# Differential attention: whole-tile splits of queries and keys, and query low parts moved by transfers

## The chip, the cores and the metric

The kernel runs on one core of a Trainium2 chip. The metric is the device time of one execution in microseconds (us). The kernel before has a median of 1926.02 us over three runs (1925.98 to 1927.47).

## The reference, cut to what matters

The reference is a decoder trunk of two layers over 512 tokens of width 1024, in float32. Each layer is: a half-step SwiGLU feed-forward, a token mixer, a cross attention into 256 memory tokens, and a second half-step feed-forward, each followed by a layer norm. The mixer of the first layer is differential attention, and the change lies in it:

```python
def diff_attention(x, w_qkv, w_o, lam_q, lam_k, subln_g, cos, sin, lam_init):
    q, k, v = jnp.split(x @ w_qkv, 3, axis=-1)
    q = q.reshape(B, S, H, 2, dk)          # 8 heads, each with 2 components of 64
    k = k.reshape(B, S, H, 2, dk)
    v = v.reshape(B, S, H, 2 * dk)
    q = rope(q, c5, s5)
    k = rope(k, c5, s5)
    ...
        s = jnp.einsum('bqhcd,bkhcd->bhcqk', qblk, k) * scale     # scale = 64 ** -0.5
        s = jnp.where(mask, s, jnp.finfo(jnp.float32).min)
        p = jax.nn.softmax(s, axis=-1)
        a = p[:, :, 0] - lam * p[:, :, 1]
        return jnp.einsum('bhqk,bkhe->bqhe', a, v)
    ...
```

Each head has two components. Each component has its own scores, from 64 columns of the query and 64 of the key; the two softmaxes are combined and multiplied with one value matrix of 128 columns.

## The kernel before

**Products in parts.** The operands of TensorE are of the type float32r, a rounded float32. To keep the reference's precision, the kernel splits a float32 operand x into a high part hi = round(x), written by ScalarE as float32r, and a low part lo = x - hi, written by VectorE. A product of two operands is then hi·hi + hi·lo + lo·hi, three matmuls in one accumulation (`mm3`, lines 201 to 208).

**The stage.** `diff_attention` (line 1205) runs in one phase. A main generator, `da_main`, goes through the heads in pairs: values of the pair, and for each head the projection of the query and of the key, 24 matmuls of 128x512 each. A side generator, `da_side`, does the attention of the heads whose query and key are ready: scores and masked exponential (`da_scores`), combination of the two softmaxes (`da_mix`), transposes of the result (`da_turn`), product with the values (`da_out`), norm and transposes of the output. `weave` (line 210) interleaves both in program order by estimated TensorE time; the scores of a head enter once the main work has gone 6000 ns past its key. From this order a planner, which walks the program with its own estimates of durations, sets the order of instructions on each engine; within an engine the order is then fixed, and an instruction that waits holds all those behind it on that engine. The DMA issues of SP are such a queue too: weight loads (L233, L266, L300) wait there for one of two raw buffers to come free.

**Rope.** A projection's result lies in PSUM with its 128 rows on the partitions: component 0 on the partitions 0 to 63 and component 1 on 64 to 127. These are the two `HALVES`. `da_rope` (L1025) takes two temporaries t1 and t2 of the tag `rt`, which has two buffers. VectorE shuffles partitions into t2 (L1028), multiplies the PSUM tile with the cosines into t1 (L1029), POOL multiplies t2 with the sines (L1030), and VectorE adds (L1031). The result t is t1.

**The query before** (`da_query`, L1034). For each component m there is one tile q[m] of the tag `qk`. ScalarE writes the scaled high part of component m in its own half (L1041). VectorE writes the low part of the same component in the other half (L1042). So q[m] holds high part over low part, 64 partitions each.

**The key before** (`da_key`, L1047). For each component, ScalarE writes the high part in its half (L1055), VectorE the low part in the same half of a tile of `low_keys` (L1056), whose other half was set to zero at the start of the stage (L1209), and ScalarE copies the high part into the other half (L1057).

**Scores before** (`da_scores`, L1060). The first product (L1070) multiplies q[m] with the doubled high key, which gives hi·hi + lo·hi in one matmul. The second (L1071) multiplies the same q[m] with the low key that is zero in one half, which gives hi·lo. So two matmuls per component replace three.

**Buffers.** The tag `qk` has 8 buffers (four tiles for each of two heads), `low` has 4 (a pair for each of two heads, taken in turn), `rt` 2, `raw` 2 (line 1577). PSUM tiles of the projections have two banks in turn, which come free when L1028 and L1029 have read them. At the end of the stage, free `qk` and `low` buffers take the split output weights (L1217).

Of the kernel before, what the change touches and what calls it, by code (L numbers as in the profile page):

```python
# [9 lines left out]
F32 = mybir.dt.float32  # L10
F32R = mybir.dt.float32r
I32 = mybir.dt.int32
AF = mybir.ActivationFunctionType
ALU = mybir.AluOpType
# [15 lines left out]
DA_DK = 64  # L30
# [10 lines left out]
HALVES = (slice(0, DA_DK), slice(DA_DK, P))  # L41
# [58 lines left out]
def drain(units):  # L100
    for _ in units:
        pass
# [7 lines left out]
class Trunk:  # L110
# [75 lines left out]
    def mm(self, name):  # L186
        return self.mmp.tile([P, S], F32, tag="mm", name=name)
# [846 lines left out]
    def da_query(self, ps):  # L1034

        nc, t = self.nc, self.da_rope(ps)
        got = [self.act("qk") for m in range(2)]
        scale = DA_DK**-0.5
        for m, q in enumerate(got):
            here, there = HALVES[m], HALVES[1 - m]  # L1040
            nc.scalar.activation(q[here], t[here], AF.Copy, scale=scale)  # L1041
            nc.vector.scalar_tensor_tensor(  # L1042
                q[there], t[here], scale, q[here].bitcast(F32), ALU.mult, ALU.subtract
            )
        return got

    def da_key(self, ps):  # L1047


        nc, t = self.nc, self.da_rope(ps)  # L1050
        his, los = [self.act("qk") for m in range(2)], self.low_keys[len(self.heads) % 2]
        for m in range(2):
            here, there = HALVES[m], HALVES[1 - m]
            hi, lo = his[m], los[m]
            nc.scalar.copy(hi[here], t[here])  # L1055
            nc.vector.tensor_sub(lo[here], t[here], hi[here].bitcast(F32))  # L1056
            nc.scalar.copy(hi[there], hi[here].bitcast(F32))  # L1057
        return his, los

    def da_scores(self, st, i):  # L1060

        nc = self.nc
        q, k, n = st["q"], st["k"], (i + 1) * P
        qi, kn = slice(i * P, n), slice(0, n)
        mx, rc, cf = self.small("mx"), self.small("rc", (P, 1)), self.small("cf", (P, 1))
        sm = st["sm"][:, i]
        sc = [self.aux("sc")[:, :n] for m in range(2)]
        mm = nc.tensor.matmul
        for m in range(2):
            mm(sc[m], q[m][:, qi], k[0][m][:, kn], start=True, stop=False)  # L1070
            mm(sc[m], q[m][:, qi], k[1][m][:, kn], start=False, stop=True)  # L1071
        p = [self.tmp("p")[:, :n] for m in range(2)]
        with self.tc.high_priority():
            for m in range(2):
                least = mx[:, m : m + 1]
                nc.vector.tensor_tensor_reduce(
                    p[m], sc[m], self.mask[:, S - n :], -1.0, -NEG, ALU.add, ALU.min, least
                )
                nc.scalar.activation(
                    p[m], p[m], AF.Exp, bias=least, scale=-1.0, accum_out=sm[:, m : m + 1]  # L1080
                )
        st["m", i] = p, sm, rc, cf
# [120 lines left out]
                yield W_E[1]  # L1203

    def diff_attention(self, layer, ln):
        self.low_keys = [self.pair("low") for i in range(2)]
        for pair in self.low_keys:
            for m, t in enumerate(pair):
                self.nc.gpsimd.memset(t[HALVES[1 - m]].bitcast(F32), 0.0)  # L1209
        self.mask = self.act("mask", (P, S), mybir.dt.bfloat16)  # L1210
        self.nc.gpsimd.memset(self.mask[:, : S - P], 0.0)
        self.nc.gpsimd.tensor_copy(self.mask[:, S - P :], self.maskr)
        self.heads, self.oT = [], [None] * DA_H
        self.weave(self.da_main(), self.da_side(), GAP)
        self.begin_ln(layer, ln, 1.0)
        home = lambda tag: lambda: self.pair(tag)
        homes = [[home("qk")] * 4, [home("low"), home("low"), home("p"), home("p")]]  # L1217
        drain(self.to_tokens(self.oT[4:], self.a["da_w_o"][0], 4, 4, False, True, ALPHA, homes))
# [355 lines left out]

    def mixer(self, layer, ln):
        if layer == 0:
            bufs = dict(low=4, rt=2, a=4, p=6, o=2, qk=8, _x=0, v=4, oT=11, mask=1)
            with self.other_pools(), self.phase_pool(("v", "v"), "rt", **bufs):
                self.diff_attention(layer, ln)
            self.close_side()  # L1580
        else:
            self.later = ExitStack()
            self.later.enter_context(self.stage_pools(4, dict(raw=2), ("wh", "wl", "mem", "p", "raw")))
            self.to_w(self.later)
            self.kvp = self.later.enter_context(self.pool("kv"))
            bufs = dict(p=4, pw=1, gb=2, _x=0, pooled=16, sq=1)
            with self.phase_pool(("gb", "gb"), "sq", **bufs):
                side = self.pool_mixer(layer, ln)
                with self.tc.high_priority():
                    self.load_memory()  # L1590
                w = self.a["xa_wkv"][layer]
                raws = [self.raw_cols(w, c) for c in (0, D)]
                self.pool_bias()
                next(side)
                self.kv, self.keys, self.kv_bufs = [], [], 10
                self.weave(self.early_kv(layer, ln, 2, raws), side, 850, 8500)
            self.close_side()
# [46 lines left out]
```

## Time and profile before

| what | value |
|---|---|
| median of three runs | 1926.02 us |
| the profiled execution | 1925.08 us |
| its span, first to last instruction | 1923.3 us |
| granted TensorE clock | 0.999 |
| the attention stage in it | about 340 to 550 us |

All times in rows of the profile are from the profiled execution, counted from the start of its span. PE is TensorE's matmuls, PEld its weight loads, DVE is VectorE, ACT ScalarE, POOL GpSimd and SP the engine whose queue issues transfers; PEld and SP with a "q" behind them are sequencers. A group's row gives line, engine, operation, output<-inputs, shapes and count; then busy us and the mean ns of one; then the idle time of the engine just before, with what ended it. A row in order of time gives start, duration (us), engine, line and operation. A row of waits gives who waited <- for whom: us in total, times, longest. Matmuls overlap each other in their pipeline, so that a busy TensorE is not one at its peak rate. Releasers are inferred.

### The profile page before, as it was taken

The numbers are of one execution on the slowest core, as the hardware profiler recorded it, in microseconds if no ns is written. First come the engines' busy times: TensorE is split into PE (matmuls) and PEld (weight loads), VectorE is DVE, ScalarE is ACT, GpSimd is POOL, SyncE is SP. The second block draws the span as 40 slices with busy tenths as digits, with TensorE's granted clock in tenths as the row PEclk, the third lists the DMA queues.
The fourth block names the chain that finished last, engine by engine and source line by source line (L and its number), as shares of the span: only waits on it lengthen the run. The fifth ranks groups of instructions, "written<-read, shape, count | busy, mean of one in ns | idle before, by whom it ended". The sixth has DMA issues, their size and how long they took to land.

```text
span 1923.3 us, 32450 instructions
## 1 busy us (share of the span) xinstructions
PE 1892.8 (98%) x13050; PEld 1737.6 (90%) x13050; DVE 1563.6 (81%) x2263; ACT 1023.1 (53%) x1580; POOL 319.7 (17%) x278
## 2 busy tenths in 40 slices
PE   8999999999999999999999999999999999999998
PEld 7999998888878888999998999999899889999997
DVE  6888989888967558889888988898787568898886
ACT  6555554567755435645554655455455436555553
POOL 2112121111210001221220311212130012111210
PEclk9999999999999999999999999999999999999999
DMA  9978772322124317977785587778334337877861
GB/s 237 221 169 187 166 148 77 91 66 88 61 94 154 110 66 193 181 179 162 144 194 175 108 179 166 179 163 184 111 132 132 132 88 160 173 170 168 185 133 55
DMA packets 246742, 277.94 MB, mean 145 GB/s; under 512 B 8256, under 2 KB 212544, under 8 KB 246592
## 3 DMA queue, kind: packets, MB, share of 16 engines
q0 software_dynamic: 92928, 92.29, 31.2%
q1 hardware_dynamic: 153664, 183.59, 29.3%
q8 instruction: 102, 1.67, 0.4%
q14 instruction: 48, 0.39, 0.1%
HBM read 273.75 MB, written 2.10 MB: 143 GB/s over the span
## 4 chain that ended last, share of the span: by engine, by line
PE 78%; DVE 13%; ACT 4%; DMA 2%; issue 2%; POOL 1%; SPq 0%; DVEq 0%; ACTq 0%; POOLq 0%
PE x L205 7%; PE x L206 7%; PE x L207 7%; PE z L207 4%; PE z L206 4%; PE z L205 4%; PE ps L205 4%; PE ps L207 4%; PE ps L206 4%; DVE wl L121 2%; PE px L205 2%; PE px L207 2%; PE px L206 2%; DMA ra<-in_ffn_w_in_dram 2%; PE y L207 2%
## 5 line engine op out<-in xcount | busy, mean ns | idle before, releaser
L666 POOL DMA_DIRECT2D ra<-in_ffn_w_in_dram x132 | 170.8, 1317 | 987.0 <-DVE wl L121 802.6
L120 ACT CAST wh<-ra 128x1024 fp32r<-128x1024 f32 x184 | 193.4, 1053 | 216.7 <-PE x L206 68.1
L121 DVE TENSOR_TENSOR wl<-ra,wh 128x1024 fp32r<-128x1024 f32 x184 | 223.7, 1221 | 72.8 <-ACT wh L120 72.2
L120 ACT CAST wh<-rc 128x1024 fp32r<-128x1024 f32 x136 | 143.0, 1053 | 116.9 <-PE x L206 41.6
L205 PE MATMUL x<-xe,wh 128*128 128x256 f32 x704 | 195.0, 277 | 0.0
L206 PE MATMUL x<-xe,wh 128*128 128x256 f32 x704 | 194.8, 277 | 0.0
L207 PE MATMUL x<-xe,wl 128*128 128x256 f32 x704 | 194.8, 277 | 0.0
L121 DVE TENSOR_TENSOR wl<-rc,wh 128x1024 fp32r<-128x1024 f32 x136 | 164.8, 1221 | 28.2 <-ACT wh L120 27.8
L120 ACT CAST wh<-b 128x1024 fp32r<-128x1024 f32 x112 | 117.8, 1052 | 128.3 <-PE x L206 65.6
L121 DVE TENSOR_TENSOR wl<-b,wh 128x1024 fp32r<-128x1024 f32 x112 | 136.9, 1222 | 39.4 <-ACT wh L120 39.1
L205 PE MATMUL x<-xh,wh 128*128 128x256 f32 x544 | 151.1, 278 | 0.0
L206 PE MATMUL x<-xl,wh 128*128 128x256 f32 x544 | 150.6, 277 | 0.0
L207 PE MATMUL x<-xh,wl 128*128 128x256 f32 x544 | 150.6, 277 | 0.0
L206 PEld LDWEIGHTS x<-xe,wh 128*128 128x128 f32 x704 | 132.5, 188 | 1.4
L205 PEld LDWEIGHTS x<-xe,wh 128*128 128x128 f32 x704 | 132.2, 188 | 1.3
L207 PEld LDWEIGHTS x<-xe,wl 128*128 128x128 f32 x704 | 132.2, 188 | 0.0
L121 DVE TENSOR_TENSOR wl<-raw,wh 128x1024 fp32r<-128x1024 f32 x64 | 82.8, 1298 | 42.9 <-ACT wh L120 42.2
L206 PEld LDWEIGHTS x<-xl,wh 128*128 128x128 f32 x544 | 102.5, 188 | 0.7
L205 PEld LDWEIGHTS x<-xh,wh 128*128 128x128 f32 x544 | 102.1, 188 | 0.7
L207 PEld LDWEIGHTS x<-xh,wl 128*128 128x128 f32 x544 | 102.2, 188 | 0.0
L207 PE MATMUL y<-xh,wl 128*128 128x256 f32 x352 | 98.5, 280 | 1.2 <-DVE wl L121 0.5
L205 PE MATMUL z<-xh,wh 128*128 128x256 f32 x352 | 97.6, 277 | 1.2 <-ACT xh L120 0.8
(429 smaller groups left out, 6265.7 us busy)
## 6 DMA issues: line engine op xcount, KB each, us to landing
ra<-in_ffn_w_in_dram POOLq DMA_DIRECT2D x132, 512.0 KB, 6.9
rc<-in_ffn_w_in_dram SPq DMA_DIRECT2D x88, 512.0 KB, 5.7
b<-in_ffn_w_out_dram SPq DMA_DIRECT2D x76, 512.0 KB, 4.7
ra<-in_ffn_w_in_dram SPq DMA_DIRECT2D x44, 512.0 KB, 5.0
rc<-in_ffn_w_in_dram POOLq DMA_DIRECT2D x44, 512.0 KB, 7.6
raw<-in_xa_wkv_dram SPq DMA_DIRECT2D x16, 1024.0 KB, 5.5
raw<-in_da_w_qkv_dram SPq DMA_DIRECT2D x16, 512.0 KB, 5.2
raw<-in_xa_wq_dram SPq DMA_DIRECT2D x8, 1024.0 KB, 5.2
```

The costliest lines, as they stand in the source:

```text
L120: self.nc.scalar.copy(hi, src),
L121: self.nc.vector.tensor_sub(lo, src, hi.bitcast(F32)),
L205: mm(out, w[0], x[0], start=start, stop=False, skip_group_check=again)
L206: mm(out, w[0], x[1], start=False, stop=False, skip_group_check=again)
L207: self.last_mm = mm(out, w[1], x[0], start=False, stop=stop, skip_group_check=again)
L666: nc.gpsimd.dma_start(t, source(*block), accum_op=ALU.add)
```

## The change

It changes how queries and keys are laid out and who writes them.

- **Query.** ScalarE writes the scaled high part of both components in one operation on all 128 partitions, into q[0]. VectorE writes the low part of both in one operation, in place of the rope's result t. ScalarE copies the high part of component 1 from q[0] to q[1]. Two transfers on SP's queue copy the high part of each component into its half of a tile of `alone`, whose other half is zero. Two more transfers move the low part of each component out of t into the other half of q[m]: 64 partitions of 512 float32, 128 KB each, from SBUF to SBUF. So q[m] holds what it held before, and `alone[m]` holds the high part of one component over (or under) zeros.
- **Key.** ScalarE writes the high part of both components into hi[0] in one operation, and VectorE the low part of both into one tile lo. ScalarE then writes the high part of component 1 into both halves of hi[1], and doubles component 0 in hi[0].
- **Scores.** The first product is as before. The second multiplies `alone[m]`, the half-empty query, with the whole low key.
- **Buffers.** The zeroed tiles are now the queries' `alone` in place of `low_keys`, two pairs as before; `qk` has 10 buffers, five tiles for each of two heads.

```diff
     def da_query(self, ps):
 
         nc, t = self.nc, self.da_rope(ps)
-        got = [self.act("qk") for m in range(2)]
-        scale = DA_DK**-0.5
-        for m, q in enumerate(got):
-            here, there = HALVES[m], HALVES[1 - m]
-            nc.scalar.activation(q[here], t[here], AF.Copy, scale=scale)
-            nc.vector.scalar_tensor_tensor(
-                q[there], t[here], scale, q[here].bitcast(F32), ALU.mult, ALU.subtract
-            )
-        return got
+        q, alone = [self.act("qk") for m in range(2)], self.alone[len(self.heads) % 2]
+        scale, lo = DA_DK**-0.5, t.bitcast(F32R)
+        nc.scalar.activation(q[0], t, AF.Copy, scale=scale)
+        nc.vector.scalar_tensor_tensor(lo, t, scale, q[0].bitcast(F32), ALU.mult, ALU.subtract)
+        nc.scalar.copy(q[1][HALVES[1]], q[0][HALVES[1]].bitcast(F32))
+        for m, hi in enumerate(q):
+            nc.sync.dma_start(alone[m][HALVES[m]].bitcast(F32), hi[HALVES[m]].bitcast(F32))
+        for m in range(2):
+            nc.sync.dma_start(q[m][HALVES[1 - m]].bitcast(F32), t[HALVES[m]])
+        return q, alone
 
     def da_key(self, ps):
 
         nc, t = self.nc, self.da_rope(ps)
-        his, los = [self.act("qk") for m in range(2)], self.low_keys[len(self.heads) % 2]
-        for m in range(2):
-            here, there = HALVES[m], HALVES[1 - m]
-            hi, lo = his[m], los[m]
-            nc.scalar.copy(hi[here], t[here])
-            nc.vector.tensor_sub(lo[here], t[here], hi[here].bitcast(F32))
-            nc.scalar.copy(hi[there], hi[here].bitcast(F32))
-        return his, los
+        hi, lo = [self.act("qk") for m in range(2)], self.act("qk")
+        nc.scalar.copy(hi[0], t)
+        nc.vector.tensor_sub(lo, t, hi[0].bitcast(F32))
+        for half in HALVES:
+            nc.scalar.copy(hi[1][half], t[HALVES[1]])
+        nc.scalar.copy(hi[0][HALVES[1]], hi[0][HALVES[0]].bitcast(F32))
+        return hi, lo
 
     def da_scores(self, st, i):
...
         for m in range(2):
-            mm(sc[m], q[m][:, qi], k[0][m][:, kn], start=True, stop=False)
-            mm(sc[m], q[m][:, qi], k[1][m][:, kn], start=False, stop=True)
+            mm(sc[m], q[0][m][:, qi], k[0][m][:, kn], start=True, stop=False)
+            mm(sc[m], q[1][m][:, qi], k[1][:, kn], start=False, stop=True)
...
     def diff_attention(self, layer, ln):
-        self.low_keys = [self.pair("low") for i in range(2)]
-        for pair in self.low_keys:
+        self.alone = [self.pair("low") for i in range(2)]
+        for pair in self.alone:
...
-            bufs = dict(low=4, rt=2, a=4, p=6, o=2, qk=8, _x=0, v=4, oT=11, mask=1)
+            bufs = dict(low=4, rt=2, a=4, p=6, o=2, qk=10, _x=0, v=4, oT=11, mask=1)
```

## The prediction

> **What bounds the kernel now.** I read the page from the top: engine totals, the chain that ended last, then the stage that the diff touches by windows, its waits, and last its instructions in order of time. First the totals and, below them, the window of the whole attention stage (340 to 550 us) and of the stretch from the first query rope to the last keys; the columns are PE, PEld, DVE, ACT and POOL busy us with their counts, the granted clock and the DMA share.
>
> ```profile
> PE 1892.8 (98%) x13050; PEld 1737.6 (90%) x13050; DVE 1563.6 (81%) x2263; ACT 1023.1 (53%) x1580; POOL 319.7 (17%) x278
> PE 78%; DVE 13%; ACT 4%; DMA 2%; issue 2%; POOL 1%; SPq 0%; DVEq 0%; ACTq 0%; POOLq 0%
> 340.00:550.00 210.00, 204.31 (x1235) 178.75 (x1234) 181.78 (x444) 140.74 (x360) 37.84 (x49) 1.00 0.25 77
> 358.00:520.00 162.00, 156.31 (x930) 136.09 (x929) 144.71 (x355) 111.37 (x282) 31.75 (x38) 1.00 0.24 72
> ```
>
> TensorE is the bound, in this stage too: of 162 us it is idle 5.7 (162.00 - 156.31). VectorE is second with 144.71 of 162 (89%). Fewer VectorE instructions can therefore return at most what TensorE still waits for. These are the waits of TensorE's matmuls in the stage (us in total, times, longest):
>
> ```profile
> PE pt L489 <- DVE p L1090: 2.6, 2, 1.4
> PE sc L1070 <- ACT po L1121: 1.5, 2, 0.8
> PE sc L1070 <- ACT qk L1057: 0.9, 2, 0.7
> PE po L1112 <- DVE a L121: 0.6, 1, 0.6
> ```
>
> 5.6 us in seven waits: 2.6 behind the mix of probabilities on VectorE, 0.9 behind the last copy of the keys, 2.1 behind other work.
>
> **The change, part by part.** The groups it touches, with count, busy us and mean ns:
>
> ```profile
> L1042 DVE SCALAR_TENSOR_TENSOR qk<-rt,qk 64x512 fp32r<-64x512 f32 x16 | 11.0, 686 | 0.5
> L1056 DVE TENSOR_TENSOR low<-rt,qk 64x512 fp32r<-64x512 f32 x16 | 11.0, 685 | 0.5
> L1031 DVE TENSOR_TENSOR rt<-rt 128x512 f32<-128x512 f32 x16 | 10.9, 681 | 1.5 <-POOL rt L1030 1.5
> L1041 ACT ACTIVATE qk<-rt 64x512 fp32r<-64x512 f32 x16 | 10.1, 630 | 8.1 <-DVE rt L1031 6.6 <-DVE rc L1088 1.2
> L1055 ACT CAST qk<-rt 64x512 fp32r<-64x512 f32 x16 | 9.9, 618 | 11.3 <-DVE rt L1031 11.1
> L1057 ACT CAST qk<-qk 64x512 fp32r<-64x512 f32 x16 | 9.9, 618 | 0.4
> ```
>
> VectorE: an operation on 64 partitions takes 0.686 us and one on 128 partitions 0.681, so a whole low part costs what a half costs. Per head two query halves become one, and two key halves become one: 32 operations become 16, 22.0 us become 11.0. VectorE gains 11.0 us.
>
> ScalarE: per head two query halves become one whole and one half copy, and the keys keep four operations (one whole, three halves). At 0.62 to 0.63 us each nothing changes. The keys are finished by the fourth operation, as before: nothing. If a whole ScalarE operation cost more than a half, the nearest 128x512 form, 0.685 for the output turns at L125, would add 0.06 x 16 = 1 us on an engine idle for 51 of 162 us.
>
> TensorE: count and shapes of the score matmuls stay; the stationary operand of the second product is another tile, and every matmul already has its own weight load (13050 of each). The zeroing at the start is of the same four tiles, on POOL. Two more qk buffers hold the fifth tile of each head. All three: nothing. The scores gain waits on DMAs. A wait that an instruction cannot hold costs one of these on TensorE's sequencer:
>
> ```profile
> L1070 PEldq EVENT_SEMAPHORE  x12: 51/51/51, 385.5 to 536.6; - x12
> ```
>
> Four moves in eight heads make at most 32 x 0.051 = 1.6 us, at least 0 where the sequencer runs ahead; I take 0, since TensorE is mostly busy with earlier work when a score is decoded, and keep 1.6 for the range.
>
> The new work is 32 transfers of 128 KB from SBUF to SBUF on SP's queue, four per head. No row shows such a transfer. The nearest rows (KB, us to landing):
>
> ```profile
> out_dram<-X SPq DMA_DIRECT2D x8, 256.0 KB, 2.1
> ident<-in_ident_dram SPq DMA_DIRECT2D x1, 64.0 KB, 1.8
> raw<-in_da_w_qkv_dram SPq DMA_DIRECT2D x16, 512.0 KB, 5.2
> ```
>
> Two things wait for them. The scores need the moved query parts, but their cover is long: the first score of head 0 starts 7.4 us after its low part is there (371.79 - 364.36, rows below). The other waiter is the temporary. The rope result t now stays occupied until the two moves of the low part have read it, where before it was free after the last VectorE operation. The tag rt has two buffers, and the key's rope needs both: its first write into the second one is the multiplication with the cosines, L1029. If a buffer is not free, VectorE stands in front of L1029 with everything queued behind it: masks, mixes, weight splits. In order of time, VectorE (start, us) for the query's low part, then the key's L1029, with the key's sum L1031 where the distance is short: heads 0, 2, 7, then the shortest and the longest of the other five, heads 5 and 4.
>
> ```profile
> 363.67 1.41 DVE L1042 SCALAR_TENSOR_TENSOR qk<-rt,qk 64x512 fp32r<-64x512 f32 x2
> 365.76 0.69 DVE L1029 TENSOR_TENSOR rt<-k,ropeC 128x512 f32<-128x512 f32 x1
> 367.64 0.68 DVE L1031 TENSOR_TENSOR rt<-rt 128x512 f32<-128x512 f32 x1
> ...
> 409.63 1.41 DVE L1042 SCALAR_TENSOR_TENSOR qk<-rt,qk 64x512 fp32r<-64x512 f32 x2
> 411.73 0.69 DVE L1029 TENSOR_TENSOR rt<-k,ropeC 128x512 f32<-128x512 f32 x1
> 413.54 0.68 DVE L1031 TENSOR_TENSOR rt<-rt 128x512 f32<-128x512 f32 x1
> ...
> 507.07 1.40 DVE L1042 SCALAR_TENSOR_TENSOR qk<-rt,qk 64x512 fp32r<-64x512 f32 x2
> 509.53 0.68 DVE L1029 TENSOR_TENSOR rt<-k,ropeC 128x512 f32<-128x512 f32 x1
> 512.49 0.68 DVE L1031 TENSOR_TENSOR rt<-rt 128x512 f32<-128x512 f32 x1
> ...
> 469.13 1.40 DVE L1042 SCALAR_TENSOR_TENSOR qk<-rt,qk 64x512 fp32r<-64x512 f32 x2
> 473.40 0.69 DVE L1029 TENSOR_TENSOR rt<-k,ropeC 128x512 f32<-128x512 f32 x1
> 454.24 0.69 DVE L1042 SCALAR_TENSOR_TENSOR qk<-rt,qk 64x512 fp32r<-64x512 f32 x1
> 459.98 0.68 DVE L1029 TENSOR_TENSOR rt<-k,ropeC 128x512 f32<-128x512 f32 x1
> ```
>
> The whole low part is done when now the first half is, 0.69 us after the start of L1042. From there to L1029 there are 1.40, 1.41 and 1.77 us in heads 0, 2 and 7, and 3.6 to 5.05 in the others. Let L be the time from the low part's end to the release of t; each head's key multiplication is late by L less that distance, if positive. Lower end: a second issue 0.5 us behind the first (0.99 us for two, below) and the 1.8 of the 64 KB row, L = 2.3, late by 0.9 + 0.9 + 0.5 = 2.3 us in all. Upper end: the four moves of a head carry 512 KB like the load that lands in 5.2, so L = 5.7, late by 12.5 in those three and about 7 in the other five (each between 0.65 and 2.1). I take L = 3.0: the two moves out of t carry 256 KB, the row with 2.1, plus 0.5 for the issue and 0.4 for the two copies ahead of them. That is 1.6 + 1.6 + 1.2 = 4.4 us of late multiplications. The sum L1031 comes 1.27, 1.20 and 2.36 us after the multiplication's end, so the keys are late by only 0.3, 0.4 and 0.
>
> One head meets a weight load on the same queue. SP's issues, then the end of head 0's keys on ScalarE and its first score:
>
> ```profile
> 363.67 0.99 SPq L266 DMA_DIRECT2D raw<-in_da_w_qkv_dram  x2
> 405.33 0.99 SPq L266 DMA_DIRECT2D raw<-in_da_w_qkv_dram  x2
> ...
> 369.64 1.26 ACT L1057 CAST qk<-qk 64x512 fp32r<-64x512 f32 x2
> 371.79 0.22 PE L1070 MATMUL sc<-qk 128*128 128x128 f32 x1
> ```
>
> The load of 363.67 lands at about 363.67 + 0.5 + 5.2 = 369.4, and head 0's moves, ready from 364.4, stand behind it: release near 369.9 instead of 367.4. The multiplication is late by 4.1, the sum by 2.8, the keys are ready at 373.7 instead of 370.9, and the score of 371.79 waits 1.9 us. Head 2's load of 405.33 has landed by 411, as its moves begin: nothing.
>
> **The sum.** Gain: one half-operation less stands ahead of the two waits on the mix, 2 x 0.69 = 1.4 us of their 2.6; the other waits stay. Loss: 1.9 in head 0, 0.4 in head 2. Net +0.9 us on the profiled execution of 1925.08 us (span 1923.3 and 1.8 around it), hence 1926.0; that execution lies 0.9 below the median of 1926.02, so 1927 us as a median. The other 9.6 us that VectorE gains are hidden under TensorE; without that cover they would count whole.
>
> The rule of the skill that speaks against the change: by the Trainium skill (SBUF — State Buffer, "Can I just issue two DMAs to hit both halves?") transfers on the two halves of the partitions hardly overlap but serialise. With that page's 196 GB/s for 64 partitions and its fixed 2 us, an estimate for four moves is 2 + 4 x 0.67 = 4.7 us, and by it the multiplications would be late by some 13 us (9.5 in the three heads, about 3 in the others). No row here moves half the partitions. That is the first rival in the page's numbers.
>
> **Rivals.** Slower, by the temporary: the four moves go one after another and t is released as late as a 512 KB load lands. At L = 5.7 VectorE stands 19.5 us, more than the 11.0 it gains. For it: 5.2 is the landing of everything that this queue carries in the stage. Against it: a sum L1031 that comes 1.2 us after the multiplication absorbs some 1.2 us per head. 19.5 - 8 x 1.2 = 10 us reach the keys: 1936 us. It decides from about L = 4, where the three short heads alone have 2.6 + 2.6 + 2.2 = 7.4 us.
>
> Faster: L stays below 2, no multiplication waits, head 0's moves get ahead of the load, and the 11.0 us of VectorE clear all waits of TensorE: 1926.0 - 5.6 = 1920.4 us. For it: the 1.8 us row and VectorE's 89%. Against it: 2.1 of the 5.6 us hang on ScalarE's squares and on a turn's low part, which keep their place.
>
> Slower, by SP's queue: the moves are placed behind a weight load that is still blocked.
>
> ```profile
> SPq L233 <- DVE wl L278: 50.5, 3, 22.6
> SPq L300 <- DVE a L121: 38.9, 2, 21.1
> ```
>
> SP does stand in front of loads for up to 22.6 us. A move behind such a wait costs the head's scores what exceeds the 7.4 us of head 0: with 15 us of blocking, 7 to 8 us in one head, 1934 us. Against it: loads so far issue when their buffer comes free and SP has nothing else, so a ready move should pass first.
>
> **How the numbers follow.** Forecast (1927, no change within 0.2%, that is 3.9 us, about what a measurement of this kernel can tell): 0.40. Slower by the temporary 0.27, by SP's queue 0.08. Faster 0.25. So faster 0.25, same 0.40, slower 0.35. The range runs from 1919, the faster case with a little reordering, to 1938, the temporary's 1936 with the 1.6 us of extra waits.
>
> **What would show it.** L1042 and L1056 with 8 instructions each of 128x512 near 0.69 us; VectorE's busy time in the stage down by about 11; ScalarE and TensorE the same. New rows qk<-rt, alone<-qk and qk<-qk on SP with 128 KB: their landing, near 2.1 or near 5, decides between forecast and first rival. VectorE waiting in front of the key's L1029 for a DMA in heads 0, 2 and 7 would show the temporary; no such wait, and fewer waits on L1090, the faster case; scores waiting for a DMA, SP's queue. The prediction is wrong if the planner orders the stage anew, so that other waits than these seven appear on TensorE.

## The result and the profile after

The changed kernel takes 1931.93 us (median of 12 runs, 1928.34 to 1933.73); the kernel before takes 1925.63 us beside it (12 runs). The ratio is 1.0025 with a 95% interval of 1.0017 to 1.0033: slower by 0.25%, some 4.8 us. (The ratio on record is not that of the two medians, which lie 6.3 us apart.) That is outside the band of "no change" that was forecast (0.2%) and inside the range. The profiled execution of the changed kernel took 1932.35 us, its span 1930.6 us.

First the totals of the changed kernel's page, and below them its windows: the whole stage and two windows of 4 us. The columns are busy us of PE, PEld, DVE, ACT and POOL, then the granted clock.

```profile
PE 1898.1 (98%) x13050; PEld 1742.1 (90%) x13050; DVE 1557.2 (81%) x2247; ACT 1023.9 (53%) x1580; POOL 322.1 (17%) x278
...
340.00:550.00 210.00, 203.11 (x1207) 177.29 (x1206) 170.50 (x416) 136.53 (x345) 37.53 (x45) 0.98 0.35 97
440.00:444.00 4.00, 3.94 (x14) 3.38 (x15) 3.07 (x12) 3.76 (x9) 0.00 (x0) 0.57 0.02 4
488.00:492.00 4.00, 3.93 (x14) 3.15 (x14) 1.12 (x5) 2.85 (x9) 0.07 (x1) 0.57 0.97 316
```

VectorE does have less to do, but in the same 210 us TensorE gets through 1207 matmuls instead of 1235, and the clock is 0.98 instead of 1.00. The 4 us windows show where the clock went: at 440 and at 488 it is 0.57. Counted as 4 x (1 - 0.57), each of the two takes 1.7 us, 3.4 us together; every other window of 4 us between 340 and 580 us stands at 1.00.

The whole operations came as drawn. By line and shape, in the stage:

```profile
L1054 DVE TENSOR_TENSOR qk<-rt,qk 128x512 fp32r<-128x512 f32 x8 | 5.5, 687 | 0.8 <-ACT qk L1053 0.7
L1040 DVE SCALAR_TENSOR_TENSOR rt<-rt,qk 128x512 fp32r<-128x512 f32 x8 | 5.5, 684 | 1.0 <-ACT qk L1039 1.0
```

Sixteen operations, 11.0 us, where 32 took 22.0. The lines moved: L1040 is the query's low part, L1054 the key's.

The waits of TensorE in the stage, and VectorE's one wait for the temporary:

```profile
PE sc L1071 <- DMA low<-qk: 3.2, 2, 2.5
PE po L1111 <- ACT a L120: 0.9, 1, 0.9
PE sc L1070 <- DVE mx L1076: 0.8, 1, 0.8
PE po L1112 <- DVE a L121: 0.6, 1, 0.6
PE pt L489 <- DVE p L1090: 0.5, 1, 0.5
PE sc L1070 <- ACT qk L1056: 0.3, 1, 0.3
...
DVE rt L1029 <- DMA qk<-rt: 0.8, 1, 0.8
```

Six groups add up to 6.3 us, where before it was 5.6. The two waits on the mix (2.6) have shrunk to one of 0.5, as hoped. A wait that was not there before is the largest: the second product of the scores (L1071) waits for a transfer into `alone` (`low` in the rows, the tag of its tiles).

How much of the difference arises in this stage? The layer norm that follows the stage has a fixed chain of work, and its L378 on VectorE serves as a mark. The last mark ahead of the stage and one behind it, before:

```profile
342.46 1.28 DVE L378 SCALAR_TENSOR_TENSOR X<-X,mean,hr 128x1024 f32<-128x1024 f32 x1 [0.51 <-ACT sp L374]
581.47 1.28 DVE L378 SCALAR_TENSOR_TENSOR X<-X,mean,v 128x1024 f32<-128x1024 f32 x1
```

and after:

```profile
342.46 1.28 DVE L378 SCALAR_TENSOR_TENSOR X<-X,mean,hr 128x1024 f32<-128x1024 f32 x1 [0.51 <-ACT sp L374]
586.84 1.28 DVE L378 SCALAR_TENSOR_TENSOR X<-X,mean,v 128x1024 f32<-128x1024 f32 x1
```

The stage has lost 5.4 us between the two. Between its marks each kernel has the same 1366 matmuls (the kernel before, then the changed one):

```profile
342.46:581.47 239.01, 231.89 (x1366) 200.73 (x1366) 199.03 (x474) 151.62 (x387) 41.09 (x53) 1.00 0.26 79
342.46:586.84 244.38, 236.06 (x1366) 203.71 (x1365) 192.86 (x458) 152.49 (x387) 42.91 (x53) 0.99 0.33 95
```

TensorE is idle for 8.3 us instead of 7.1 (the length less the busy time), and busy for 4.2 us longer, most of which is the 3.4 us of half clock. So the wait for `alone` has partly taken the place of other waits.

Some 2 us more of this one execution are lost at 741 us, where TensorE waits 2.7 us for work of the feed-forward (`PE ps L205 <- DVE X L357`; 0.6 us before). No changed instruction runs there, and in a second profiled execution of the same kernel that wait was 1.5 us, so I leave it out. Below, "the stage" of a run is this difference of marks against the profiled execution of the kernel before, from one profiled execution each.

### The wait for `alone`

TensorE and SP's issues around the longest wait of the changed kernel, in order of time:

```profile
481.50 0.62 PE L1070 MATMUL sc<-qk 128*128 128x512 f32 x2
485.27 0.33 PE L1070 MATMUL sc<-qk 128*128 128x128 f32 x1
488.07 0.70 PE L1071 MATMUL sc<-qk,low 128*128 128x512 f32 x2 [2.48 <-DMA low<-qk]
489.00 0.73 PE L205 MATMUL k<-xh,wh 128*128 128x512 f32 x1
```

```profile
485.76 0.46 SPq L1043 DMA_DIRECT2D low<-qk  x1
486.33 0.53 SPq L300 DMA_DIRECT2D raw<-in_da_w_o_dram  x1
488.69 0.46 SPq L1043 DMA_DIRECT2D low<-qk  x1
```

A score of 512 keys (block 3 of a head) starts at 481.50, and its second product comes only when a transfer issued at 485.76 has landed, 2.3 us later. This score is of head 4, and the transfer is head 6's. The program says why. Two pairs of `alone` are taken in turn, so heads 4 and 6 share one. The order of the program here is: query of head 6, block 3 of head 4, block 0 of head 5, key of head 6, block 1 of head 5, query of head 7, blocks 2 and 3 of head 5, key of head 7. In the kernel before, the low keys, which then used these tiles, were written at the key, behind those blocks. `alone` is written at the query, ahead of block 3 of head 4 and of blocks 2 and 3 of head 5. The second products of these three blocks therefore wait for the later head's high part and multiply that. The amount of work is the same, but the small term high query times low key is wrong there in the changed kernel; the first experiment puts this right too.

### The profile page after: what moved, and what is told of

Same layout as the page of the kernel before. It is cut to its first block, busy times and chain, and to the rows that moved or that the text cites. A ratio compares the mean times of both kernels' runs of the same rounds, so it can differ in the third digit from the quotient of the medians.

```text
span 1930.6 us, 32524 instructions
## 1 busy us (share of the span) xinstructions
PE 1898.1 (98%) x13050; PEld 1742.1 (90%) x13050; DVE 1557.2 (81%) x2247; ACT 1023.9 (53%) x1580; POOL 322.1 (17%) x278
## 4 chain that ended last, share of the span: by engine, by line
PE 78%; DVE 14%; ACT 4%; DMA 2%; issue 2%; POOL 1%; SPq 0%; DVEq 0%; ACTq 0%; POOLq 0%
PE x L206 6%; PE x L205 6%; PE x L207 6%; PE z L206 4%; PE z L207 4%; PE z L205 4%; PE ps L205 4%; PE ps L207 4%; PE ps L206 4%; DVE wl L121 3%; PE px L205 2%; PE px L207 2%; PE px L206 2%; PE y L207 2%; PE x L681 1%
## 5 line engine op out<-in xcount | busy, mean ns | idle before, releaser
L205 PE MATMUL x<-xe,wh 128*128 128x256 f32 x704 | 195.0, 277 | 0.0
L205 PE MATMUL x<-xh,wh 128*128 128x256 f32 x544 | 151.1, 278 | 0.0
L205 PEld LDWEIGHTS x<-xe,wh 128*128 128x128 f32 x704 | 132.2, 188 | 1.3
L205 PEld LDWEIGHTS x<-xh,wh 128*128 128x128 f32 x544 | 102.2, 188 | 0.7
L206 PE MATMUL z<-xl,wh 128*128 128x256 f32 x352 | 97.5, 277 | 0.7 <-DVE xl L121 0.7
```

The lines of the kernel that those rows point to most:

```text
L205: mm(out, w[0], x[0], start=start, stop=False, skip_group_check=again)
L206: mm(out, w[0], x[1], start=False, stop=False, skip_group_check=again)
```

## The experiments

Four theories stood against each other. The *temporary*: t is held until the moves have read it, so that the key's rope comes late. The *turn* of `alone`: the late transfer of the rows above. The *traffic*: 32 more transfers cost, wherever they are. And the *whole operations*: they bring little or nothing. In all runs the times stand against the kernel before on the same chip. Line numbers shift by one in some of them.

### Transfers into `alone` behind the key

The two transfers of each head are written at the end of `da_key`, so that all reads of the earlier head come first in the program. Beside it the changed kernel ran again.

```diff
 def da_query(self, ps):
-        for m, hi in enumerate(q):
-            nc.sync.dma_start(alone[m][HALVES[m]].bitcast(F32), hi[HALVES[m]].bitcast(F32))
+        self.fill = [(alone[m], hi, HALVES[m]) for m, hi in enumerate(q)]
 def da_key(self, ps):
+        for a, h, half in self.fill:
+            nc.sync.dma_start(a[half].bitcast(F32), h[half].bitcast(F32))
         return hi, lo
```

> Edit on the changed kernel: the two transfers that copy the high part of the query into the half-empty tile are written behind the key's operations instead of behind the query's. Nothing else moves. Theory T (turn of the half-empty tiles): in the program's order the query of head h stands ahead of the last score blocks of head h-2 (head 4 block 3, head 5 blocks 2 and 3), which read the same tile of two in turn; they wait for the new head's transfer, TensorE pauses 2.5 us and 0.8 us, and its clock then runs at half speed for 3.4 us. T expects no wait of L1071's matmuls on a transfer, no stretch of clock near 0.5 around 488 us, and 2.5 + 0.8 + 1.7 = 5 us less than the changed kernel: a ratio to the kernel before between 0.998 and 1.0008. Rival M (the moves themselves: the late release of the rope's temporary and traffic on SP's queue, as the prediction had it) expects the ratio to stay at 1.0025, within 0.0008.

Measured: 1927.81 us, ratio 1.0009 (1.0 to 1.0018); stage +1.3 us.

> The changed kernel once more, for another profiled execution on the same chip. In it the second products of head 4 block 3 and of head 5 blocks 2 and 3 take the high part of the query of the head two further on, by the order told in e1. Theory T expects the wait of 2.5 us near 488 us and the half-speed stretch behind it again, as they follow from the order; the other shift seen in its first profile, 2.1 us near 740 us behind a late weight load of the next stage, may be absent. Ratio 1.0017 to 1.0033.

Measured: 1932.11 us, ratio 1.0029 (1.0017 to 1.004); stage +5.4 us, with the wait of 2.4 us at 488 and a clock of 0.57 at 440 and 488 again. So the loss of the stage repeats, and mending the turn takes away 4.1 us of its 5.4. TensorE's waits of the first kernel:

```profile
PE po L1112 <- ACT a L120: 1.5, 1, 1.5
PE pt L489 <- DVE a L121: 1.4, 2, 0.9
PE sc L1071 <- ACT qk L1055: 1.4, 2, 1.1
PE sc L1071 <- ACT qk L1056: 0.2, 1, 0.2
```

None is on a transfer any more, but 1.6 us are on the keys' copies (L1055, L1056) where before it was 0.9, and the clock still falls once (0.62 at 488 and 0.95 at 492, 1.7 us together). The keys are late, which points to the temporary but does not yet show it.

### Without the moves of the low part

The first experiment without its two moves out of t. The product of the query's low part with the key is left out of the computation; ScalarE's copy fills the other half, so that all matmuls stay.

```diff
-        nc.scalar.copy(q[1][HALVES[1]], q[0][HALVES[1]].bitcast(F32))
+        nc.scalar.copy(q[1], q[0].bitcast(F32))
...
-            nc.sync.dma_start(q[m][HALVES[1 - m]].bitcast(F32), t[HALVES[m]])
```

> Edit on the kernel of e1: the two moves of the query's low part into the other half of q are left out, and the copy of the high part to q[1] covers all 128 partitions, so that the tile is written. Left out of the computation: the product of the query's low part with the key. Rival M expects it to be faster than e1 by at least 3 us, since the temporary is free at once and SP's queue has 16 transfers less. Theory T expects the same time as e1 within 2 us (0.1%).

Measured: 1921.82 us, ratio 0.9974 (0.9965 to 0.9983); stage -4.2 us. Against the first experiment (+1.3) the moves cost 5.5 us of the stage, and without them the whole operations win. Whether they cost by holding the temporary or as traffic, this run does not tell.

### The turn alone, in the kernel before

The kernel before, with two transfers of zeros per query into the half of `low_keys` that is zero anyway: the same sizes and the same place in the program as the changed kernel's transfers, without any change of the operations. A small operation of ScalarE ties the zeros to the query's high part.

```diff
+        nc.scalar.mul(self.zero[:, :16], got[1][:, :16].bitcast(F32), 0.0)
+        for m, low in enumerate(self.low_keys[len(self.heads) % 2]):
+            there = HALVES[1 - m]
+            nc.sync.dma_start(low[there].bitcast(F32), self.zero[there].bitcast(F32))
         return got
```

> Edit on the kernel before: at the end of each query two transfers of 128 KB copy zeros over the zero half of the low-key tiles whose turn it is; their source depends on the query by a tiny ScalarE operation (128x16, 8 times). VectorE's half operations, the rope's temporary and the keys stay as before. Theory T expects that this alone brings the waits: blocks 2 and 3 of late heads wait for the next-but-one head's transfer, TensorE pauses over 1.5 us at least once and its clock halves; 2 to 6 us slower than before, ratio 1.001 to 1.003. Rival M expects no change, ratio 0.9992 to 1.0008, since no temporary is held and the scores' own transfers land 2.3 us after issue, long before they are used.

Measured: 1933.4 us, ratio 1.0033 (1.0021 to 1.0046); stage +7.6 us. Its wait and its clock:

```profile
PE sc L1075 <- DMA low<-zero: 3.0, 2, 1.6
...
488.00:492.00 4.00, 1.30 (x5) 0.72 (x4) 1.65 (x4) 2.28 (x7) 1.26 (x1) 0.82 0.79 252
492.00:496.00 4.00, 4.00 (x13) 3.22 (x13) 2.69 (x9) 2.36 (x7) 0.43 (x2) 0.50 0.00 0
496.00:500.00 4.00, 4.00 (x18) 3.40 (x17) 3.14 (x12) 3.31 (x12) 0.00 (x0) 0.82 0.00 0
```

The turn makes a kernel slower that has nothing else of the change but as many transfers as go into `alone` (and eight small operations of ScalarE). Of its 7.6 us 3.0 are the waits and 3.4 the half clock (4 x (0.18 + 0.50 + 0.18)); the two overlap by some 0.5 us, since by the windows' clock the slow stretch begins in the last 1.1 us of a wait.

### The temporary: three buffers, another queue, another engine, a buffer of its own

All four start from the first experiment. First, the tag `rt` with three buffers and `oT` with ten to make room:

```diff
-            bufs = dict(low=4, rt=2, a=4, p=6, o=2, qk=10, _x=0, v=4, oT=11, mask=1)
+            bufs = dict(low=4, rt=3, a=4, p=6, o=2, qk=10, _x=0, v=4, oT=10, mask=1)
```

> Edit on the kernel of e1: the rope's temporary gets a third buffer (rt=3); the output tiles give one of their eleven for it (oT=10). The third buffer lets the key's rope start without waiting for the moves out of the query's temporary. e2 without low moves was 0.35% faster than e1. Theory B (the moves cost by holding the temporary) expects most of this back: ratio to the kernel before 0.997 to 0.9990. Rival Q (they cost by traffic: SP's issues and weight loads late behind them) expects the ratio of e1, 1.0009, within 0.0008.

Measured: 1935.77 us, ratio 1.0042 (1.0029 to 1.0055), yet the stage is at -3.6 us. The loss comes behind it, in one wait of the next stage, and its load had been issued late:

```profile
590.36 1.87 PE L1348 MATMUL pt<-ident,p 128*128 128x128 f32 x5 [9.21 <-DMA p<-in_mem_dram]
...
584.96 2.14 SPq L1335 DMA_DIRECT2D p<-in_mem_dram  x4
```

Before, that load was issued at 554.31. By its time as a whole this run would have cleared the temporary of blame; its stage convicts it. Why the load came late was not tried; that the third buffer moved the addresses of the tiles behind it is only an argument.

Second, the moves of the low part on POOL's queue:

```diff
-            nc.sync.dma_start(q[m][HALVES[1 - m]].bitcast(F32), t[HALVES[m]])
+            nc.gpsimd.dma_start(q[m][HALVES[1 - m]].bitcast(F32), t[HALVES[m]])
```

> Edit on the kernel of e1: the two moves of the query's low part are issued on POOL's queue instead of SP's. The temporary is held as long as before or longer. Rival Q expects the gain here, a ratio of 0.997 to 0.9990, since SP's queue holds only loads and the high copies. Theory B expects no gain, 1.0005 or more, and slower if the software queue lands later than 2.7 us.

Measured: 1937.73 us, ratio 1.0052 (1.0038 to 1.0066); stage +11.4 us. Here the first rival of the prediction appears as it was drawn, VectorE standing in front of L1029, and TensorE in front of the key's projection. In head 0 the two moves landed 5.0 and 6.7 us after their issue, where the median of the 16 is 2.7; why they landed late was not tried.

```profile
DVE rt L1029 <- DMA qk<-rt: 9.8, 4, 4.3
...
PE k L205 <- DVE rt L1029: 4.0, 2, 3.3
```

Third, the low parts moved by ScalarE, with no transfer out of t:

```diff
-            nc.sync.dma_start(q[m][HALVES[1 - m]].bitcast(F32), t[HALVES[m]])
+            nc.scalar.copy(q[m][HALVES[1 - m]], t[HALVES[m]])
```

> Edit on the kernel of e1: the two moves of the query's low part are ScalarE copies of 64x512 between the halves, 16 of about 0.62 us, in place of transfers; the computation is complete. The temporary is free 1.3 us after the low part. Theory B expects a ratio of 0.997 to 0.9995, as in e2 apart from 9.9 us more on ScalarE, which is idle for a third of the stage. A rival S, that ScalarE's 9.9 us come into the chain of scores, exponentials and splits, expects 1.000 to 1.003.

Measured: 1926.62 us, ratio 0.9995 (0.9986 to 1.0004); stage -1.0 us. Better than by transfers from a shared buffer by 2.3 us of the stage, but no better than the kernel before beyond its interval. That the 16 more operations on ScalarE take the rest of the gain is likely, but not shown.

Fourth, the query's rope result in a buffer of its own, tag `tq`, at the price of one `oT` buffer. All 32 transfers stay on SP's queue.

```diff
-    def da_rope(self, ps):
+    def da_rope(self, ps, tag="rt"):
-        t1, t2 = self.tmp("rt"), self.tmp("rt")
+        t1, t2 = self.tmp(tag), self.tmp("rt")
...
-        nc, t = self.nc, self.da_rope(ps)
+        nc, t = self.nc, self.da_rope(ps, "tq")
...
-            bufs = dict(low=4, rt=2, a=4, p=6, o=2, qk=10, _x=0, v=4, oT=11, mask=1)
+            bufs = dict(low=4, rt=2, a=4, p=6, o=2, qk=10, _x=0, v=4, oT=10, tq=1, mask=1)
```

> Edit on the kernel of e1: the query's rope result gets a buffer of its own (tag tq, one buffer), which takes the place of the eleventh output tile, so that all other tiles keep their addresses; the third buffer of e5 had shifted them, and behind the stage TensorE waited 9.2 us there for the next stage's memory tokens, while the attention stage itself was 3.5 us shorter than before. All transfers stay. Theory B (the moves cost by holding the temporary) expects the stage of e5 without that wait: the key's cosine multiplication 0.6 to 1.3 us behind its shuffle in all heads, the stage 3 to 4 us shorter than before the change, ratio 0.9975 to 0.9990. Rival Q (the transfers' traffic) expects the ratio of e1, 1.0009.

Measured: 1923.98 us, ratio 0.9983 (0.9974 to 0.9992); stage -3.5 us, clock 1.00 throughout. This version beats both kernels. Against the first experiment the buffer alone is worth 4.8 us of the stage. All transfers are still there, so that the traffic of the 16 moves as such costs about 0.7 us at most (-3.5 here, -4.2 without the moves), which the two ratios do not tell apart.

How the temporary acts shows in VectorE's order. The key's shuffle and its L1029, changed kernel, heads 0 (with the query's low part, L1040, ahead of it, and the weight splits, L278, between them) and 6:

```profile
363.55 0.68 DVE L1040 SCALAR_TENSOR_TENSOR rt<-rt,qk 128x512 fp32r<-128x512 f32 x1
364.30 0.74 DVE L1028 STREAM_SHUFFLE rt<-k 128x512 f32<-128x512 f32 x1
365.13 2.38 DVE L278 TENSOR_TENSOR wl<-raw,wh 128x512 fp32r<-128x512 f32 x2
367.51 0.69 DVE L1029 TENSOR_TENSOR rt<-k,ropeC 128x512 f32<-128x512 f32 x1
...
491.91 0.74 DVE L1028 STREAM_SHUFFLE rt<-k 128x512 f32<-128x512 f32 x1
497.86 0.67 DVE L1029 TENSOR_TENSOR rt<-k,ropeC 128x512 f32<-128x512 f32 x1
```

and with the buffer of its own:

```profile
364.75 0.74 DVE L1028 STREAM_SHUFFLE rt<-k 128x512 f32<-128x512 f32 x1
365.38 0.68 DVE L1029 TENSOR_TENSOR rt<-k,ropeC 128x512 f32<-128x512 f32 x1
...
487.28 0.74 DVE L1028 STREAM_SHUFFLE rt<-k 128x512 f32<-128x512 f32 x1
487.91 0.67 DVE L1029 TENSOR_TENSOR rt<-k,ropeC 128x512 f32<-128x512 f32 x1
```

From shuffle to multiplication it is 3.2 and 5.95 us in the one, 0.63 in the other. Over the eight heads the distances add up to 33.7 us in the changed kernel, 6.5 before, 27.5 in the first experiment, 5.8 with the own buffer. VectorE hardly waits for the moves in the changed kernel (0.8 us): other work, such as L278 in head 0, stands in front of L1029, as the planner orders by its own estimate of when the buffer comes free. The loss is an order, not a wait of VectorE.

### The own buffer in the changed kernel

The same `tq` with the transfers into `alone` where the change has them.

> Edit on the changed kernel: the query's own temporary as in e9, with the high copies where the change has them. In it the second products of head 4 block 3 and of head 5 blocks 2 and 3 take the high part of the query of the head two further on. If the two causes are independent and add, it stands above e9 by what e1 took away, 0.16 to 0.20%: ratio 0.9990 to 1.0012, with a wait of scores for the high copies again. If the late temporary was what made that wait matter, it equals e9 within 0.0008.

Measured: 1924.71 us, ratio 0.9989 (0.998 to 0.9998); stage -2.7 us. Its waits:

```profile
PE sc L1071 <- DMA low<-qk: 2.8, 2, 2.5
PE pt L489 <- ACT o L1137: 1.1, 1, 1.1
PE sc L1070 <- ACT qk L1057: 0.5, 1, 0.5
```

The turn's wait is as long as in the changed kernel, but the clock stays at 1.00 and the turn costs only 0.8 us of the stage (-2.7 against -3.5), within the intervals of the two ratios. TensorE's idle time between the marks grows by no more than 0.4 us (4.9 against 4.5): the wait for the transfer has taken the place of other waits. By the stages the two losses don't add: with the temporary held, the turn costs 4.1; with it free, 0.8. By the ratios it is 0.16 to 0.20% against 0.06%, which intervals of 0.09% to either side do not tell apart.

### Keys alone

The first experiment with the query by half-operations as before, and no moves out of t; the high parts still go into `alone` by transfers, and the keys are written by whole operations.

```diff
+            nc.scalar.activation(hi[here], t[here], AF.Copy, scale=scale)
+            nc.vector.scalar_tensor_tensor(
+                hi[there], t[here], scale, hi[here].bitcast(F32), ALU.mult, ALU.subtract
+            )
```

> Edit on the kernel of e1: the query is written as before the change, by half operations of ScalarE and VectorE (VectorE has 8 half operations more than in e1, 5.5 us), with no low moves; the high copies into the half-empty tiles stay transfers, and the keys and scores stay as changed. The computation is complete. Theory B expects the gain of e2 less at most the 5.5 us of VectorE: 0.9975 to 1.0000. If the high copies cost as much as the low moves (rival Q), 1.000 to 1.002.

Measured: 1924.04 us, ratio 0.9984 (0.9975 to 0.9993); stage -1.9 us. Half of VectorE's gain (5.5 us), with no temporary held, gives about half of what the whole gives with its own buffer. By the runs' ratios the two cannot be told apart.

### The runs together

"Half clock" is an estimate, the sum of 4 x (1 - clock) over the stage's 4 us windows.

| kernel | ratio | stage, us | half clock in it, us | without it, us |
|---|---|---|---|---|
| changed | 1.0025 | +5.4 | 3.4 | +1.9 |
| turn mended (first experiment) | 1.0009 | +1.3 | 1.7 | -0.5 |
| temporary mended | 0.9989 | -2.7 | 0 | -2.7 |
| both mended | 0.9983 | -3.5 | 0 | -3.5 |
| turn mended, no moves of low parts | 0.9974 | -4.2 | 0 | -4.2 |
| before, with the turn | 1.0033 | +7.6 | 3.4 | +4.1 |

From both mended to the changed kernel it is 8.9 us of the stage. Read down, the temporary is worth 8.1 with the turn present and 4.8 without it; 3.4 and 1.7 of these are half clock.

## Why the prediction was right and wrong

It gave 1927 us with "no change within 0.2%" as the most likely case; measured were 1931.93 us and 0.25% slower. The range held, partly by luck: gain and loss of the sum were both too small, 1.4 us against 3.5 and 2.3 against 8.9, and these errors offset each other in part. The case that it names its first rival, slower by the temporary, had the right cause for one of the two losses: the runs show 4.8 to 8.1 us where it has 10. But in the changed kernel VectorE does not stand and wait, as it has it; the work is ordered anew.

- **VectorE gains 11.0 us; ScalarE and TensorE nothing.** Right: 16 operations of 0.684 and 0.687 us, 11.0 us less; score matmuls as before.
- **"Gain: one half-operation less stands ahead of the two waits on the mix, 2 x 0.69 = 1.4 us".** Nearly right for these two waits and too small for the stage. With both losses mended the waits on the mix fall from 2.6 to 1.4 us, but the stage gains 3.5, and 4.2 without the moves. That "the other waits stay" was the error. Between the marks TensorE's idle time falls from 7.1 to 4.5 us: the waits on L1121 (1.5) and L1112 (0.6) are gone, and 1.1 us in smaller ones are new. Another 0.8 us is less busy time of TensorE for the same matmuls, for which I have no cause. The faster rival's 5.6 us lie as far above the 3.5 as the forecast's 1.4 lie below.
- **"The scores need the moved query parts, but their cover is long".** This step failed, and it is the main one. The 7.4 us of head 0 are a distance in time between a head's own parts and its own scores. What waited was the score of the head two before it, on the same pair of tiles. Such a wait follows from the order of the program and the turn of the buffers, and no row of the profile before could give it; it stood in the diff, where `low_keys` is written at the key and `alone` at the query. It is worth 4.1 us in the changed kernel (5.4 to 1.3), 1.7 of them half clock.
- **L = 3.0, "1.6 + 1.6 + 1.2 = 4.4 us of late multiplications", "the keys are late by only 0.3, 0.4 and 0".** L was right for heads 0 and 2 alone. A move lands 2.3 us (into `alone`) or 2.7 us (out of t) after its issue (medians of 16), and in head 0 the low part is done at 364.23 and L1029 starts at 367.51, so that t was free at most 3.3 us later. From the low part's end to the landing of the second move out of t, L is 3.1 to 3.2 us in heads 0 and 2, 3.7 in head 4, 4.2 to 4.8 in heads 1, 3 and 7, and some 7.5 in heads 5 and 6. There the moves go behind the 1024 KB loads issued at 468.73 and 486.33 and land 6.0 and 4.5 us after their issue; in head 6 they also stand on SP behind a transfer into `alone` that waits for ScalarE's copy (L1041) until 488.66. So the first rival's condition, L of about 4 or more, held in five heads of eight. (Its price was a little low: at L = 5.7 the rows before give 8.2 us for the five other heads, not about 7.) And the distances from shuffle to L1029 grew by 33.7 - 6.5 = 27.2 us in all, in seven heads of eight and not in three, because the planner ordered the stage anew. I had taken the distances of the order before as fixed cover. The temporary costs 4.8 to 8.1 us of the stage, against the forecast's 2.3.
- **Head 0, 1.9 us behind a weight load.** Wrong, as SP's issues in the changed kernel show:

```profile
363.18 1.16 SPq L1043 DMA_DIRECT2D low<-qk  x2
364.38 1.24 SPq L1045 DMA_DIRECT2D qk<-rt  x2
365.73 1.27 SPq L266 DMA_DIRECT2D raw<-in_da_w_qkv_dram  x2
```

  All four transfers go ahead of the load. What was forecast for head 0, moves landing late behind a load, came in heads 5 and 6. The rival of SP's queue, moves behind a load that is still blocked, did not come: the moves out of t are issued at most 0.9 us after the low part's end, and 2.6 us after it in head 6, where the copy of ScalarE holds the queue.
- **"The prediction is wrong if the planner orders the stage anew, so that other waits than these seven appear on TensorE".** That is what happened. By the Trainium skill (SBUF — State Buffer, "Can I just issue two DMAs to hit both halves?") the estimate for the four moves was 4.7 us. In head 0 it is 4.2 us from the first issue (363.18) to the last landing, a little below it.
- **What no step had: the clock.** 3.4 of the stage's 5.4 us are, by the estimate above, matmuls at half clock behind pauses.

The traffic of the transfers as the main cause is refuted by the own buffer's run, which keeps all 32 and gains. Not settled are the 2 us that the profiled execution lost at 741 us, and the late load of the run with three buffers.

## What to carry to other kernels

A transfer that reads a compute temporary holds it until it has landed, here 2.7 us after its issue for 128 KB (median of 16) and up to 6.1 behind a weight load, and this kernel's planner then moved what needs the buffer: give such a result a buffer of its own before counting what the faster operation brings. When the writer of a tile that is taken in turn moves to another place in the program, list in the program's order who still has to read the earlier contents; distances in time from the old trace don't show it. Such a move can also change what is read, as it did here. Look at marks around the stage as well as at the total: one run here was 0.42% slower with a stage that was 3.6 us faster.

## What the runs showed of the hardware that was not expected

Short pauses of TensorE were followed by 3.4 us at half clock. In the changed kernel, two waits of 0.93 and 0.64 us close together:

```profile
439.03 0.39 PE L1111 MATMUL po<-v,a 128*128 128x256 f32 x1 [0.93 <-ACT a L120]
440.06 0.33 PE L1112 MATMUL po<-v,a 128*128 128x128 f32 x1 [0.64 <-DVE a L121]
440.45 0.64 PE L205 MATMUL q<-xh,wh 128*128 128x512 f32 x1
440.89 0.63 PE L206 MATMUL q<-xl,wh 128*128 128x512 f32 x1
```

From 440.45 to 443.88, matmuls of 128x512 start every 0.43 us instead of every 0.23. In the kernel before with the turn the slow stretch is twice as long (6.9 us, from the three windows shown there). In the run on POOL's queue a longer pause had no such effect (a wait, and the window behind it at clock 1.00):

```profile
372.96 0.47 PE L205 MATMUL k<-xh,wh 128*128 128x512 f32 x1 [3.27 <-DVE rt L1029]
...
376.00:380.00 4.00, 3.77 (x21) 3.38 (x22) 3.15 (x11) 3.34 (x9) 1.09 (x2) 1.00 0.10 22
```

The Trainium skill (TensorE: Matmul & The Clock Gate, "Why this matters for your kernels") asks for no idle gap over about 3 us. Here pauses below that length did it, and one above it did not, so length alone does not decide; that page's window of activity ("What's actually happening"), free-running and about 3.4 us long, would fit the length of the slow stretch, but no run here shows its phase. Which pause drops the clock stays open: the wait of 2.5 us at 488 does it in the changed kernel, and a wait as long in the kernel with the own buffer alone does not.
